# Weighted sum of two experts' outputs: tiles of 12 tokens with whole-tile vector work, and tiles of 16 tokens worked token by token

## The chip, the core and the metric

The kernel runs on one core of a Trainium2 chip. The core has several engines that run their own instruction streams side by side. Three of them matter here: VectorE (DVE in the profile), ScalarE (ACT) and SyncE (SP), which does no arithmetic and issues transfers. Transfers between the chip's memory (HBM) and the core's working memory (SBUF, 128 partitions) are carried out by 16 DMA engines, whichever engine issued them. Transfers that SP issues stand in queue q1 of the profile, those that ACT issues in q10.

The metric is device time in microseconds (us) of one execution; lower is better.

## What is computed

For each of 16 x 1024 = 16,384 tokens there are two vectors of 512 floats (the outputs of two experts) and two weights. The result is the weighted sum of the two vectors:

```python
batch, seq, hidden, n_experts, k = 16, 1024, 512, 8, 2
"expert_outputs": np.random.randn(batch, seq, k, hidden).astype(np.float32),
"combine_weights": np.random.randn(batch, seq, k).astype(np.float32),

def reference(expert_outputs, combine_weights):
    weights = combine_weights[..., np.newaxis]
    return np.sum(expert_outputs * weights, axis=2).astype(np.float32)
```

Every input element is read once and every output element written once: 67.2 MB in, 33.6 MB out. A token is 4 KB of input and 2 KB of output.

## The kernel before

The 16,384 tokens are spread over 128 partitions, so each partition owns `per` = 128 tokens. `rows` (line 34) splits them: the first `main` = 120 tokens of a partition lie next to each other in HBM, and the remaining `LAST` = 8 lie in a second block. A tile `et` (line 63) holds J = 12 tokens of each partition, both expert vectors of a token side by side: 48 KB a partition. The pool has four such buffers. The loop over g runs 11 times: ten tiles of 12 tokens and a last one of 8.

The work is done in place. `ot` (line 65) is a view of the front half of the tile's own memory, in which the sums are packed densely, so that a store reads one contiguous run of each partition. A buffer is free for a new load only when the store out of it is done.

Loads are issued by SP (line 69). The first tile is loaded in two pieces, 2 and 10 tokens; `max_dma_last_dim` cuts the first piece into rows of 4 KB. The weights `wt` are loaded once, in two pieces, by ACT (line 55). `warm` (line 60) is one small product on ACT that takes the load of ACT's function table out of the way early.

There are three forms of compute:

- Tiles 0 to 8 (lines 76 to 81): one DVE multiplication of the whole tile by the weights, repeated along each vector (`wb`), 12,288 elements a partition (line 78), then one DVE addition of the two halves, 6,144 elements (line 79). ACT issues the store (line 80).
- Tile 9 (lines 84 to 88 and 98 to 103): ACT makes the first expert's products, token by token (line 86); DVE multiplies the second expert's vectors (line 101) and adds (line 102). SP issues the store (line 103).
- Tile 10, the 8 tokens: for each token ACT makes the first product (line 86), and DVE multiplies the second vector by its weight and adds in one instruction, `scalar_tensor_tensor` (line 90). SP issues the store (line 103).

The engines are kept in step by semaphores that the framework inserts. It also sets the order in which each engine's instructions are issued, which is not always that of the source: in the profile, SP issues the last tile's load (line 69) before tile 9's store (line 103), and ACT's first product of tile 9 stands ahead of tile 8's store (line 80).

Of the kernel before, what the change touches and what calls it, by code (L numbers as in the profile page):

```python
# [1 line left out]

# [4 lines left out]


@with_exitstack
def kernel(  # L10
    ctx: ExitStack,
    tc: tile.TileContext,
    expert_outputs: bass.AP,
    combine_weights: bass.AP,
    out: bass.AP,
):

    nc = tc.nc  # L20
    b, s, k, h = expert_outputs.shape
    assert k == 2
    n = b * s
    P = nc.NUM_PARTITIONS
    per = n // P
    assert per * P == n
    J, LAST = 12, 8
    main = per - LAST
    assert main % J == 0
    eo = expert_outputs.rearrange("b s k h -> (b s) (k h)")  # L30
    cw = combine_weights.rearrange("b s k -> (b s) k")
    o = out.rearrange("b s h -> (b s) h")

    def rows(x):

        a = x[0 : P * main, :].rearrange("(p t) f -> p t f", p=P)
        b = x[P * main : n, :].rearrange("(p t) f -> p t f", p=P)
        return lambda t, c: a[:, t : t + c, :] if t < main else b[:, t - main : t - main + c, :]

    eo, cw, o = rows(eo), rows(cw), rows(o)  # L40

    dt = mybir.dt.float32
    mult = mybir.AluOpType.mult
    add = mybir.AluOpType.add
    copy = mybir.ActivationFunctionType.Copy

    last = main // J

    wpool = ctx.enter_context(tc.tile_pool(name="w", bufs=1))
    ipool = ctx.enter_context(tc.tile_pool(name="in", bufs=4))  # L50

    wt = wpool.tile([P, per * k], dt)

    for t, c in ((0, main), (main, LAST)):
        nc.scalar.dma_start(
            out=wt[:, k * t : k * (t + c)].rearrange("p (t k) -> p t k", k=k), in_=cw(t, c)
        )

    warm = wpool.tile([P, 1], dt)
    nc.scalar.activation(out=warm, in_=nc.const_aps.tensor(1.0, (P, 1), dt), func=copy)  # L60

    for g in range(last + 1):
        et = ipool.tile([P, J, k * h], dt)

        ot = et.rearrange("p j f -> p (j f)")[:, 0 : J * h].rearrange("p (j f) -> p j f", f=h)
        t0, c = g * J, J if g < last else LAST

        for a, m in ((0, 2), (2, c - 2)) if g == 0 else ((0, c),):
            nc.sync.dma_start(  # L69
                out=et[:, a : a + m],  # L70
                in_=eo(t0 + a, m),
                max_dma_last_dim=k * h * 4 if g + a == 0 else None,
            )
        if g < last - 1:

            wb = wt[:, g * J * k : (g + 1) * J * k].unsqueeze(2).to_broadcast([P, J * k, h])
            ek = et.rearrange("p j (k h) -> p (j k) h", k=k)
            nc.vector.tensor_tensor(out=ek, in0=ek, in1=wb, op=mult)  # L78
            nc.vector.tensor_tensor(out=ot, in0=et[:, :, 0:h], in1=et[:, :, h : 2 * h], op=add)  # L79
            nc.scalar.dma_start(out=o(t0, c), in_=ot)  # L80
            continue


        for i in range(c):
            t = t0 + i
            nc.scalar.activation(  # L86
                out=et[:, i, 0:h], in_=et[:, i, 0:h], func=copy, scale=wt[:, 2 * t : 2 * t + 1]
            )
            if g == last:
                nc.vector.scalar_tensor_tensor(  # L90
                    out=ot[:, i, :],
                    in0=et[:, i, h : 2 * h],
                    scalar=wt[:, 2 * t + 1 : 2 * t + 2],
                    in1=et[:, i, 0:h],
                    op0=mult,
                    op1=add,
                )
        if g < last:
            w1 = wt.rearrange("p (t k) -> p t k", k=k)[:, t0 : t0 + c, 1:2]
            x1 = et[:, :, h : 2 * h]  # L100
            nc.vector.tensor_tensor(out=x1, in0=x1, in1=w1.to_broadcast([P, c, h]), op=mult)  # L101
            nc.vector.tensor_tensor(out=ot, in0=et[:, :, 0:h], in1=x1, op=add)  # L102
        nc.sync.dma_start(out=o(t0, c), in_=ot[:, 0:c])


# [1 line left out]
_INS = ['expert_outputs', 'combine_weights']  # L107
_OUTS = [((16, 1024, 512), 'float32')]


# [23 lines left out]
```

## Time and profile before

The median of three runs is 239.04 us (239.02 to 239.04). The profiled execution has a span of 237.3 us from the first to the last instruction.

| | |
|---|---|
| median of the runs | 239.04 us |
| span of the profiled execution | 237.3 us |
| DVE multiplication of a whole tile (line 78) | 9 x 12.96 us |
| DVE addition of a whole tile (line 79) | 9 x 6.56 us |
| ACT product of one token (line 86) | 20 x 0.707 us |
| DVE multiply-add of one token (line 90) | 8 x 0.748 us |
| load of 12 tokens (6 MB), issue to landing, median | 29.9 us |
| store of 12 tokens (3 MB) from ACT, issue to landing, median | 32.7 us |
| last store (2 MB), issue to landing | 10.0 us |

A DMA transfer of a tile is cut into packets, one for each contiguous run of a partition: 128 packets, eight for each of the 16 DMA engines. The "DMA share" of the profile is the mean busy share of these 16 engines. The page also follows back a chain of waits from the last instruction; in it the DMA has 59% of the span (30% in loads, 29% in stores), DVE 33% and ACT 2%. Idle time of an engine that does not set the end costs nothing.

### The profile page before, as it was taken

The page shows a single profiled execution, that of the slowest core. Times are in us where ns is not written, and L with a number is a line of the kernel's source. Part 1 is how long each engine was busy: PE and PEld are TensorE (multiplying, and loading weights), DVE is VectorE, ACT ScalarE, POOL GpSimd, SP SyncE. Part 2 cuts the span into 40 slices and gives each one's busy share as a digit, 9 for nine tenths or more (in the row PEclk, how much of TensorE's full clock was granted, in tenths as well). Part 3 has the DMA queues.
Part 4 walks back from the last instruction along what each step waited for, and adds up shares of the span by engine and source line. Part 5 has one row for each costly group of instructions (what it writes and reads, how often), then busy time and mean ns, then how long its engine had stood idle before and what let it go on. Part 6 is the DMA issues. An engine that isn't in the chain of part 4 may idle for free.

```text
span 237.3 us, 154 instructions
## 1 busy us (share of the span) xinstructions
DVE 193.9 (82%) x28; ACT 14.0 (6%) x22; POOL 0.2 (0%) x4
## 2 busy tenths in 40 slices
DVE  0008999999999999999999879969996998785710
ACT  2000000000000000000000000000000000740800
POOL 0000000000000000000000000000000000000000
DMA  8999999989899999999897999999997979999997
GB/s 308 443 456 406 398 431 497 398 356 505 356 439 435 427 464 464 398 398 522 348 522 344 452 427 435 464 464 398 398 522 340 530 336 460 458 403 442 402 438 309
DMA packets 3728, 100.80 MB, mean 425 GB/s; under 512 B 528, under 2 KB 656, under 8 KB 912
## 3 DMA queue, kind: packets, MB, share of 16 engines
q1 hardware_dynamic: 2144, 72.35, 71.1%
q10 hardware_dynamic: 1584, 28.44, 27.9%
HBM read 67.24 MB, written 33.55 MB: 425 GB/s over the span
## 4 chain that ended last, share of the span: by engine, by line
DMA 59%; DVE 33%; ACT 2%; DVEq 0%; ACTq 0%; issue 0%; SPq 0%
DMA et<-in_expert_outputs_dram 30%; DMA out_dram<-et 29%; DVE et L78 22%; DVE et L79 11%; ACT et L86 2%; DVE et L90 1%; DVEq L129 0%; ACTq L129 0%; SPq L69 0%; DVEq L78 0%; ACTq L86 0%
## 5 line engine op out<-in xcount | busy, mean ns | idle before, releaser
L78 DVE TENSOR_TENSOR et<-et,wt 128x12288 f32<-128x12288 f32 x9 | 116.6, 12955 | 25.2 <-DMA et<-in_expert_outputs_dram 25.2
L79 DVE TENSOR_TENSOR et<-et 128x6144 f32<-128x6144 f32 x9 | 59.0, 6558 | 0.3
L86 ACT ACTIVATE et<-et,wt 128x512 f32<-128x512 f32 x20 | 12.5, 707 | 209.2 <-DMA et<-in_expert_outputs_dram 209.2
L90 DVE SCALAR_TENSOR_TENSOR et<-et,wt 128x512 f32<-128x512 f32 x8 | 5.6, 748 | 3.9 <-ACT et L86 3.7
L101 DVE TENSOR_TENSOR et<-et,wt 128x6144 f32<-128x6144 f32 x1 | 6.6, 6559 | 2.3 <-DMA et<-in_expert_outputs_dram 2.3
L102 DVE TENSOR_TENSOR et<-et 128x6144 f32<-128x6144 f32 x1 | 6.6, 6559 | 0.9 <-ACT et L86 0.9
L60 ACT ACT_TABLE_LOAD x1 | 1.3, 1283 | 1.7 <-issue 1.7
L60 ACT ACTIVATE warm<-const-float32-1.0 128x1 f32<-128x1 f32 x1 | 0.2, 202 | 0.0
L118 POOL MEMSET const-bfloat16-1.0<- 128x1 bf16 x1 | 0.1, 102 | 0.0
L118 POOL MEMSET const-uint8-127<- 128x1 uint8 x1 | 0.1, 102 | 0.0
L118 POOL MEMSET const-float32-0.0<- 128x1 f32 x1 | 0.1, 99 | 0.2 <-issue 0.2
L118 POOL MEMSET const-float32-1.0<- 128x1 f32 x1 | 0.1, 99 | 0.0
## 6 DMA issues: line engine op xcount, KB each, us to landing
et<-in_expert_outputs_dram SPq DMA_DIRECT2D x9, 6144.0 KB, 29.9
out_dram<-et ACTq DMA_DIRECT2D x9, 3072.0 KB, 32.7
et<-in_expert_outputs_dram SPq DMA_DIRECT2D x1, 5120.0 KB, 17.3
et<-in_expert_outputs_dram SPq DMA_DIRECT2D x1, 4096.0 KB, 25.1
out_dram<-et SPq DMA_DIRECT2D x1, 3072.0 KB, 14.6
out_dram<-et SPq DMA_DIRECT2D x1, 2048.0 KB, 10.0
et<-in_expert_outputs_dram SPq DMA_DIRECT2D x1, 1024.0 KB, 5.4
wt<-in_combine_weights_dram ACTq DMA_DIRECT2D x1, 120.0 KB, 4.4
```

The lines of the kernel that those rows point to most:

```text
L60: nc.scalar.activation(out=warm, in_=nc.const_aps.tensor(1.0, (P, 1), dt), func=copy)
L78: nc.vector.tensor_tensor(out=ek, in0=ek, in1=wb, op=mult)
L79: nc.vector.tensor_tensor(out=ot, in0=et[:, :, 0:h], in1=et[:, :, h : 2 * h], op=add)
L86: nc.scalar.activation(out=et[:, i, 0:h], in_=et[:, i, 0:h], func=copy, scale=wt[:, 2 * t : 2 * t + 1])
L90: nc.vector.scalar_tensor_tensor(out=ot[:, i, :], in0=et[:, i, h : 2 * h], scalar=wt[:, 2 * t + 1 : 2 * t + 2], in1=et[:, i, 0:h], op0=mul ...
L101: nc.vector.tensor_tensor(out=x1, in0=x1, in1=w1.to_broadcast([P, c, h]), op=mult)
L102: nc.vector.tensor_tensor(out=ot, in0=et[:, :, 0:h], in1=x1, op=add)
L118: nc = _bacc.Bacc("TRN2", target_bir_lowering=False, num_devices=1)
```

## The change

The tile becomes 16 tokens (64 KB a partition), and the pool has three buffers, so that the tiles take the same memory, 192 KB a partition. The loop runs 8 times, over tiles of the same size. All tiles are computed in one form, that of the old last tile: for each token one ACT product and one DVE multiply-add, both in place. A helper, `combine`, does this for c tokens from token a of the tile and returns the dense view to store.

The first tile is still loaded in two pieces, now 2 and 14 tokens, and stored in one. The last tile is loaded in pieces of 12 and 4 tokens, and each piece is computed and stored by itself. The second block of `rows` holds 16 tokens a partition in place of 8. Stores of all tiles but the last are issued by ACT, those of the last by SP.

```diff
-    J, LAST = 12, 8
-    main = per - LAST
-    assert main % J == 0
+    J = 16
+    PIECES = (12, 4)
+    assert sum(PIECES) == J and per % J == 0
+    main = per - J
...
-    ipool = ctx.enter_context(tc.tile_pool(name="in", bufs=4))
+    ipool = ctx.enter_context(tc.tile_pool(name="in", bufs=3))
...
+    def combine(et, a, c, t0):
+
+        ot = et[:, a : a + c].rearrange("p j f -> p (j f)")[:, 0 : c * h]
+        ot = ot.rearrange("p (j f) -> p j f", f=h)
+        for i in range(c):
+            t = t0 + a + i
+            x = et[:, a + i]
+            nc.scalar.activation(
+                out=x[:, 0:h], in_=x[:, 0:h], func=copy, scale=wt[:, 2 * t : 2 * t + 1]
+            )
+            nc.vector.scalar_tensor_tensor(
+                out=ot[:, i, :],
+                in0=x[:, h : 2 * h],
+                scalar=wt[:, 2 * t + 1 : 2 * t + 2],
+                in1=x[:, 0:h],
+                op0=mult,
+                op1=add,
+            )
+        return ot
+
+    last = per // J - 1
     for g in range(last + 1):
         et = ipool.tile([P, J, k * h], dt)
-
-        ot = et.rearrange("p j f -> p (j f)")[:, 0 : J * h].rearrange("p (j f) -> p j f", f=h)
-        t0, c = g * J, J if g < last else LAST
-
-        for a, m in ((0, 2), (2, c - 2)) if g == 0 else ((0, c),):
+        t0 = g * J
+        if g == 0:
+            loads, stores = ((0, 2), (2, J - 2)), ((0, J),)
+        elif g < last:
+            loads = stores = ((0, J),)
+        else:
+            loads = stores = ((0, PIECES[0]), (PIECES[0], PIECES[1]))
+        for a, c in loads:
             nc.sync.dma_start(
...
-        if g < last - 1:
-
-            wb = wt[:, g * J * k : (g + 1) * J * k].unsqueeze(2).to_broadcast([P, J * k, h])
-            ek = et.rearrange("p j (k h) -> p (j k) h", k=k)
-            nc.vector.tensor_tensor(out=ek, in0=ek, in1=wb, op=mult)
-            nc.vector.tensor_tensor(out=ot, in0=et[:, :, 0:h], in1=et[:, :, h : 2 * h], op=add)
-            nc.scalar.dma_start(out=o(t0, c), in_=ot)
-            continue
...
+        for a, c in stores:
+            ot = combine(et, a, c, t0)
+            (nc.sync if g == last else nc.scalar).dma_start(out=o(t0 + a, c), in_=ot)
```

More of the change, by code (lines that the diff above doesn't have):

```diff
@@ L45 @@
     copy = mybir.ActivationFunctionType.Copy
-    last = main // J
     wpool = ctx.enter_context(tc.tile_pool(name="w", bufs=1))
-    ipool = ctx.enter_context(tc.tile_pool(name="in", bufs=4))
+    ipool = ctx.enter_context(tc.tile_pool(name="in", bufs=3))
     wt = wpool.tile([P, per * k], dt)
-    for t, c in ((0, main), (main, LAST)):
+    for t, c in ((0, main), (main, J)):
         nc.scalar.dma_start(
@@ L69 @@
             nc.sync.dma_start(
-                out=et[:, a : a + m],
-                in_=eo(t0 + a, m),
-                max_dma_last_dim=k * h * 4 if g + a == 0 else None,
-            )
-        if g < last - 1:
-            wb = wt[:, g * J * k : (g + 1) * J * k].unsqueeze(2).to_broadcast([P, J * k, h])
-            ek = et.rearrange("p j (k h) -> p (j k) h", k=k)
-            nc.vector.tensor_tensor(out=ek, in0=ek, in1=wb, op=mult)
-            nc.vector.tensor_tensor(out=ot, in0=et[:, :, 0:h], in1=et[:, :, h : 2 * h], op=add)
-            nc.scalar.dma_start(out=o(t0, c), in_=ot)
-            continue
@@ L84 @@
[L84 to L103, printed above, removed]
+                out=et[:, a : a + c],
+                in_=eo(t0 + a, c),
+                max_dma_last_dim=k * h * 4 if t0 + a == 0 else None,
+            )
```

## The prediction

> **What bounds the kernel now.** I read the page first, and in it the DMA before the engines. DVE is busy 82% of the span, which looks like the bound; the DMA row says otherwise.
>
> ```profile
> span 237.3 us, 154 instructions
> DVE 193.9 (82%) x28; ACT 14.0 (6%) x22; POOL 0.2 (0%) x4
> DMA  8999999989899999999897999999997979999997
> DMA packets 3728, 100.80 MB, mean 425 GB/s; under 512 B 528, under 2 KB 656, under 8 KB 912
> q1 hardware_dynamic: 2144, 72.35, 71.1%
> q10 hardware_dynamic: 1584, 28.44, 27.9%
> ```
>
> The two queues together fill 71.1 + 27.9 = 99.0% of sixteen DMA engines' time: 234.9 us of 237.3. Both move bytes at one rate (72.35 MB in 0.711 x 237.3 = 168.7 us is 429 GB/s, 28.44 MB in 66.2 us is 430), so reads and writes draw on one budget. Second, I looked in the windows for where the missing 2.4 us lie.
>
> ```profile
> core 0: us, DVE busy (x) ACT busy (x) POOL busy (x), PEclk, DMA share, GB/s
> 0.00:1.00 1.00, 0.00 (x0) 0.00 (x0) 0.20 (x4) 1.00 0.00 0
> 1.00:2.00 1.00, 0.00 (x0) 0.26 (x1) 0.00 (x0) 1.00 0.40 61
> ...
> 234.00:235.00 1.00, 0.00 (x0) 0.00 (x0) 0.00 (x0) 1.00 1.07 459
> 235.00:236.00 1.00, 0.00 (x0) 0.00 (x0) 0.00 (x0) 1.00 0.62 262
> 236.00:237.00 1.00, 0.00 (x0) 0.00 (x0) 0.00 (x0) 1.00 0.00 0
> ```
>
> They lie at the two ends: nothing moves in the first microsecond nor after about 236. (Single windows scatter around 1, since a packet is counted where it ends.) Third, the timeline shows that DVE waits for the DMA in the second half, not the reverse:
>
> ```profile
> 137.66 12.96 DVE L78 TENSOR_TENSOR et<-et,wt 128x12288 f32<-128x12288 f32 x1 [2.17 <-DMA et<-in_expert_outputs_dram]
> ...
> 159.43 12.96 DVE L78 TENSOR_TENSOR et<-et,wt 128x12288 f32<-128x12288 f32 x1 [2.21 <-DMA et<-in_expert_outputs_dram]
> ...
> 217.04 9.79 SPq L103 DMA_DIRECT2D out_dram<-et  x2
> 219.93 5.01 ACT L86 ACTIVATE et<-et,wt 128x512 f32<-128x512 f32 x8 [9.51 <-DMA et<-in_expert_outputs_dram]
> 220.69 5.78 DVE L90 SCALAR_TENSOR_TENSOR et<-et,wt 128x512 f32<-128x512 f32 x8 [3.67 <-ACT et L86]
> ```
>
> Tiles start 21.77 us apart. The trace's packet records give the cause: a 49,152-byte load packet takes 1.815 us and a 24,576-byte store packet 0.912 (medians), each transfer has 128 packets, 8 per engine, and 8 x (1.815 + 0.912) = 21.82. So the kernel is a DMA stream without holes, and a change gains only by moving bytes in less time, and loses only by opening a hole.
>
> **The DMA work after the change.** Packet medians by size: 4,096 bytes 0.159 us, 16,384 0.611, 24,576 0.912, 32,768 1.213, 40,960 1.514, 49,152 1.815: each 8,192 bytes cost 0.301. My estimates from that step for sizes not in the trace: 57,344 bytes 2.116, 65,536 bytes 2.417, 8,192 bytes 0.310. Per engine:
>
> Loads before: 9 x 8 x 1.815 + 8 x 1.514 + 8 x 1.213 = 152.5 us. After: 6 x 8 x 2.417 + 8 x 2.116 + 8 x 1.815 + 8 x 0.611 = 152.4. The first two tokens (256 packets of 4,096 bytes) are the same in both.
> Stores before: 10 x 8 x 0.912 + 8 x 0.611 = 77.8. After: 7 x 8 x 1.213 + 8 x 0.912 + 8 x 0.310 = 77.7.
>
> Unrounded the two give -0.13 and -0.14: fewer, longer packets save **0.27 us**. The one size I can bound only loosely is 65,536. If such a row is cut in two, each half is 1.213 and the 48 rounds cost 48 x 0.009 = 0.4 us more; on the other side nothing under the byte rate is to be had. I take the uncut 2.417, as three equal steps in a row point to it. The weights' two small loads stay.
>
> **The compute**, costed at nothing, with the cover named. Removed are nine pairs of 12.96 + 6.56 = 19.5 us on DVE and one tile in mixed form. Added are 120 more pairs of the form that the old last tile has: 707 ns on ACT, 748 on DVE, overlapped. Eight of them took 226.47 - 219.93 = 6.5 us from the first product to the last sum, that is about 0.8 + 0.72 a token. A tile of 16 takes 0.8 + 16 x 0.72 = 12.4 us. Its cover is the tile's DMA time, 8 x (2.417 + 1.213) = 29.0 us. Without that cover, the excess over 29.0 would be paid seven times. ACT now carries products and store issues: seven stores wait in ACT's queue for the tile's last sum, and behind each stand the next tile's 16 products. Those are not due until the next load lands, some 29 us after the last one, so a wait of under a microsecond for DVE costs nothing. Four transfers fewer are issued (23 to 19, beside the weights), at about 0.34 us of SP's or ACT's time each, in which these engines would wait anyway.
>
> **Three buffers in place of four.** Both hold 48 tokens. A buffer's round is load, compute, store, and two delays. The first store, issued at 38.22, landed at 64.07 (from the trace's semaphore times): 25.85 us against 21.8 of shared packets, so about 4 us beyond; with 64 KB packets I put 6. After: 29 + 12.4 + 29 + 6 = 76 against the 3 x 29.0 = 87 that the stream needs. Before: 21.8 + 19.5 + 21.8 + 4 = 67 against 87. The spare time falls from 20 to 11 us and stays positive. The tightest place is load 3: tile 0 lands at 18.5 + 4 x 1.21 = 23.4, store 0 is issued at 34, lands at about 34 + 29 + 6 = 69, and load 2 lands at about 71. If load 3 is a little late, store 1, ready since 56, fills the engines alone for 9.7 us.
>
> **The tail** decides. If the stream has no hole, the last landing is 236.50 - 0.27 = 236.2. The two last stores hold 7.3 + 2.5 = 9.8 us, so the 4-token load and store 6 are through at 226.4. They hold 4.9 + 9.7 = 14.6 us, so if the two run side by side the 12-token load has landed by about 213. Its sums are done 0.8 + 12 x 0.72 = 9.5 later, at 222.5; a transfer needs about 1.1 us from issue to its first bytes (0.73 to 1.8 at the kernel's start), so store 12 is there at 223.6, 2.8 us before the engines would run dry. The 4-token load lands at 226.4, its sums are done 0.8 + 2.9 later, store 4 is there at 231.2, and store 12 keeps the engines busy to 233.7: 2.5 us spare. So the tail costs 0. The other bound: were store 6 half through before the 12-token load ends, that load would land 4.8 us later, at 217.7, and a hole of 2.0 us would open. I take 0, as store 6 queues behind store 5, which shares the rings with loads till near that point.
>
> **Sum.** 237.30 - 0.27 = 237.03 of span. The measured median exceeds the span by 239.04 - 237.30 = 1.74, which I carry over: **238.8 us**, 0.1% less.
>
> Two rules of the Trainium skill speak against this. The last store is 1 MiB. The nearest row is the old last store, 2 MiB, which landed 4.84 us after the store ahead of it, its packets' 8 x 0.611 and no more. The page "DMA: Bandwidth & Descriptors", section "Bandwidth", has 1 MB alone at 6.15 us, 78% of peak; by it the end would come about 3.7 us later, at 242.4. That figure is for a lone transfer, and here the ring is full. And the page "ScalarE: Activation LUTs", "Rules for kernel authors", sends multiplications to VectorE. Rows: 707 ns on ACT against 12,955 / 24 = 540 on DVE. With the rule a token would cost DVE 0.54 + 0.72 us, twelve 15.9, and store 12 would come about 3.6 us late: 242.4 too.
>
> **Rivals.**
> A, *product and sum take turns* (slower). Products and sums write into one tile, in place; were each product held until the sum before it, a token would cost 0.707 + 0.748 = 1.455 us, twelve 17.5. Store 12 would be there at 212.8 + 17.5 + 1.1 = 231.4, 5 us after the engines ran dry: 243.8. It decides from 12.3 us for the 12 tokens (1.0 a token, against 0.8 now); a milder slowing of the pairs opens the same hole in part. Against it: the eight pairs of the old last tile ran in 6.5 us and not 11.6. 15%, with the tail's other bound.
> B, *stores issued behind the next tile's products* (the issue order isn't the source's). For it: the ninth store was issued at 203.26, after the tenth tile's first product at 202.96, though its sum ended at 200.68. A store that waits for the next landing makes a buffer's round 29 + 29 + 29 + 6 = 93 against 87: up to 2 us a tile over five tiles, 248. Against: in the old kernel that delay cost the DMA nothing, and now sums end 16 us ahead of the next load. 4%.
> C, *a better stream* (faster). The packets of 49,152 average 1.823, not 1.815, as some 20 took up to 2.42 when the first store began: 1152 x 0.0084 / 16 = 0.6 us. If that vanishes, 238.2. Nothing in the change removes a first store. 20%.
> D, *64 KB rows cut in two*: 239.2, inside the forecast's class.
>
> **How the numbers follow.** About 0.2% (0.48 us) is what a measurement here tells from no change. Forecast with D: 61%, hence same 0.61; faster 0.20 from C; slower 0.19 from A and B. The likeliest time is 238.8, its own range 238.5 to 239.3. The range at 8 in 10 goes down to C's 238.2 and up to 240.6, a hole of 1.8 us in the tail, near its other bound.
>
> **What would show it.** Queue shares that again sum to 99%, DVE near 40%, DVE waiting for the DMA ahead of every tile, sums at about 0.72 us spacing, and no window under 0.8 in the last 25 us. A hole between the last load and the first tail store shows A; store issues after the next tile's first product, B. A busy sum of loads and stores below 234 us would break the byte arithmetic itself.

## The result, and the profile after

The changed kernel takes 242.25 us (median of 4 runs, 242.21 to 242.41) against 239.04 (239.02 to 239.08): 1.0136 times as long, 95% interval 1.0122 to 1.0150. It is 1.4% slower; 238.8 was forecast, and 240.6 was the upper end of the range. The profiled execution took 242.21 us with a span of 240.4, so that the span, too, grew by 3.1 us.

The page of the changed kernel, in the same lines that were read before:

```profile
span 240.4 us, 412 instructions
...
DVE 87.2 (36%) x128; ACT 81.0 (34%) x130; POOL 0.2 (0%) x4
...
DMA  9989989899999999898999999999989999999895
...
DMA packets 3155, 100.82 MB, mean 419 GB/s; under 512 B 464, under 2 KB 592, under 8 KB 848
...
q1 hardware_dynamic: 1856, 71.30, 69.4%
q10 hardware_dynamic: 1296, 29.49, 28.5%
q14 instruction: 3, 0.02, 0.0%
```

Three things are to be seen. DVE's share fell from 82% to 36%, as it should. The two data queues hold 97.9% of sixteen engines' time where they held 99.0%. And there is a queue that the page of before did not have: q14, of the kind "instruction", with three packets. Instructions, too, are fetched through the DMA engines: the kernel with 412 of them on its page has such fetches during the run, the one with 154 had none.

Then the costliest groups:

```profile
L68 DVE SCALAR_TENSOR_TENSOR et<-et,wt 128x512 f32<-128x512 f32 x128 | 87.2, 746 | 146.4 <-ACT et L65 144.6
L65 ACT ACTIVATE et<-et,wt 128x512 f32<-128x512 f32 x128 | 79.5, 708 | 149.6 <-DMA et<-in_expert_outputs_dram 149.6
```

The columns behind the bars are busy time, mean ns of one, idle time before them and what ended it. Both operations have the length forecast, and ACT stood idle for 149.6 us, all of it for loads. The compute is hidden.

The end of the timeline, with start, duration, engine, line and, in brackets, the idle time before:

```profile
205.62 0.34 ACTq L96 DMA_DIRECT2D out_dram<-et  x1
217.93 7.46 ACT L65 ACTIVATE et<-et,wt 128x512 f32<-128x512 f32 x12 [14.25 <-DMA et<-in_expert_outputs_dram]
218.68 8.43 DVE L68 SCALAR_TENSOR_TENSOR et<-et,wt 128x512 f32<-128x512 f32 x12 [13.09 <-ACT et L65]
227.13 6.86 SPq L96 DMA_DIRECT2D out_dram<-et  x2
229.74 2.56 ACT L65 ACTIVATE et<-et,wt 128x512 f32<-128x512 f32 x4 [4.36 <-DMA et<-in_expert_outputs_dram]
230.50 3.12 DVE L68 SCALAR_TENSOR_TENSOR et<-et,wt 128x512 f32<-128x512 f32 x4 [3.39 <-ACT et L65]
```

The 12-token load is in at 217.9, not 213, and its store is issued at 227.13. The windows around that (busy time of each engine, then the clock, the DMA share and GB/s):

```profile
core 0: us, DVE busy (x) ACT busy (x) POOL busy (x), PEclk, DMA share, GB/s
225.00:226.00 1.00, 1.00 (x3) 0.39 (x1) 0.00 (x0) 1.00 1.04 442
226.00:227.00 1.00, 1.00 (x2) 0.00 (x0) 0.00 (x0) 1.00 0.39 164
227.00:228.00 1.00, 0.10 (x1) 0.00 (x0) 0.00 (x0) 1.00 0.35 147
228.00:229.00 1.00, 0.00 (x0) 0.00 (x0) 0.00 (x0) 1.00 1.36 557
```

Between 226 and 228 the DMA engines are a third busy: a hole of about 1.2 us per engine. The timeline places it ahead of the arrival of the store of the 12 tokens, issued at 227.13.

So far this looks like the "other bound" of the tail. The trace's semaphore events show more. Each transfer raises its semaphore sixteen times, once for each DMA engine that has finished its part; the time of a transfer is that of the last of the sixteen. (The Trainium skill's "DMA: Bandwidth & Descriptors", "Why a DMA increments its semaphore by 16 and not by 1", says that the engines finish independently and that each posts its own increment; the sixteen separate times here agree.) Landing of the last store of each kernel, in us:

| | before | after |
|---|---|---|
| first of sixteen | 236.05 | 238.17 |
| fifteenth | 236.46 | 238.34 |
| sixteenth | 236.50 | 239.42 |

After the change, fifteen engines finish together and one 1.08 us later. The "mean of sixteen engines" that the prediction worked with hides this: one late engine sets the end, and the other fifteen only wait for it. Where that engine lost its time can be followed in the packet records and in the sixteen events of each load:

- *Fetches.* The three q14 packets of 8,192 bytes start at 84.82, 111.55 and 227.70 us and take 0.309 each; the data packet that follows each of them on its DMA engine takes 0.53, 0.24 and 0.64 us longer than its size does elsewhere. After the first, the last of the sixteen events of each load stands 0.97 us further behind the first of them (3.42 us, from 2.45). The third comes while the last load is under way, and that load's sixteenth event is 1.73 behind the fifteenth (0.87 in the load before). The second hits another engine. DVE's instruction stream, 207 entries with its waits, stands at its 71st entry at the first fetch and at its 196th at the third; ACT's at its 67th at the second. So the first and the third are taken for DVE's, the second for ACT's.
- *The start of the second ring* (a ring: the packets of one queue that wait on a DMA engine; q1 and q10 have one each). While the first store begins among loads in flight, at 34 to 44 us, 31 load packets of 65,536 bytes take 2.5 to 3.9 us in place of 2.418, 1.23 us per engine; before it was 19 to 22 packets of 49,152 and 0.56 to 0.6. And it hits engines unevenly: from then on four engines have their part of each load some 1.9 us later than the other twelve, where before all sixteen lay within 0.46. (Their part of each store comes some 1.3 us earlier; so a part of this is another order of the same work, and only the rest is lag.)
- *The byte arithmetic* gives 0.27 back, as forecast.

The trace does not name the engine of a packet, but most packets can be put in sixteen rows, as one begins where another ends. One row holds both of DVE's fetches; it has no gap up to its end at 238.99, where the other fifteen rows end between 237.84 and 237.97. For this late engine, -0.27, the two fetches with the packets behind them (0.84 and 0.95), and the difference at the ring's start (1.23 - 0.56 = 0.67 on the mean; 1.75 - 0.56 = 1.19 for its own row) make 2.2 to 2.7 of the 2.92 us by which the last landing moved. The hole is not in this sum: it shows as idle time of 0.5 to 1.9 us in the fifteen other rows, and the late one has work all through it. That fetches make one engine late and this engine sets the end was the theory (**F**, for fetch) that went into the experiments; **H**, that the hole explains the loss, was its rival.

### The profile page after: what moved, and what is told of

Same layout as the page of the kernel before. It is cut to its first block, busy times and chain, and to the rows that moved or that the text cites. A ratio compares the mean times of both kernels' runs of the same rounds, so it can differ in the third digit from the quotient of the medians.

```text
span 240.4 us, 412 instructions
## 1 busy us (share of the span) xinstructions
DVE 87.2 (36%) x128; ACT 81.0 (34%) x130; POOL 0.2 (0%) x4
## 4 chain that ended last, share of the span: by engine, by line
DMA 85%; DVE 6%; ACT 4%; issue 1%; SPq 1%; DVEq 0%; ACTq 0%
DMA et<-in_expert_outputs_dram 54%; DMA out_dram<-et 30%; DVE et L68 6%; ACT et L65 4%; SPq L89 1%; DVEq L122 0%; DVEq L68 0%; ACTq L65 0%
## 5 line engine op out<-in xcount | busy, mean ns | idle before, releaser
L68 DVE SCALAR_TENSOR_TENSOR et<-et,wt 128x512 f32<-128x512 f32 x128 | 87.2, 746 | 146.4 <-ACT et L65 144.6
L65 ACT ACTIVATE et<-et,wt 128x512 f32<-128x512 f32 x128 | 79.5, 708 | 149.6 <-DMA et<-in_expert_outputs_dram 149.6
```

The costliest lines, as they stand in the source:

```text
L65: nc.scalar.activation(out=x[:, 0:h], in_=x[:, 0:h], func=copy, scale=wt[:, 2 * t : 2 * t + 1])
L68: nc.vector.scalar_tensor_tensor(out=ot[:, i, :], in0=x[:, h : 2 * h], scalar=wt[:, 2 * t + 1 : 2 * t + 2], in1=x[:, 0:h], op0=mult, op1=add,)
```

## The experiments

The kernel before ran beside each of them. Its 90 runs there spread from 238.9 to 240.9 us (59 of them at 239.4 or less), so that the intervals, which are all against the kernel before, are wider than in the first comparison. The changed kernel itself did not run beside them, so a difference from its 242.25 has no interval.

**Is it the hole?** The last tile in pieces of 8, 4 and 4 closes it.

```diff
-    PIECES = (12, 4)
+    PIECES = (8, 4, 4)
...
-            loads = stores = ((0, PIECES[0]), (PIECES[0], PIECES[1]))
+            loads = stores = ((0, 8), (8, 4), (12, 4))
```

> The changed kernel with its last tile loaded, made and stored as 8, 4 and 4 tokens instead of 12 and 4. Theory H (a hole in the tail): in the changed kernel most DMA engines lie idle for some 0.5 to 1.6 us from about 226.5, until the store of 12 tokens arrives, which had to wait for the landing of 12 tokens and their 9 us of sums. With 8 tokens first, that store is ready some 6 us earlier and the hole closes: last landing 1.2 us earlier, about 241.0 us against 242.25. Rival F (the end is set by one DMA engine that instruction fetches have put about 1 us behind, and the idle time of the other fifteen costs nothing): no change, 242.1 to 242.4.

Measured 242.18 us (1.0112 times before, 1.0074 to 1.0151). Its windows, in the same columns:

```profile
225.00:230.00 5.00, 2.39 (x4) 1.71 (x4) 0.00 (x0) 1.00 0.98 408
230.00:235.00 5.00, 2.91 (x4) 2.12 (x4) 0.00 (x0) 1.00 0.94 400
```

The hole is gone and the time is the same. The last store lands at 239.27, its sixteenth event 0.93 behind the fifteenth. H, which expected 1.2 us less, falls: as long as an engine is late, the hole costs little or nothing. (This profile also has two losses more than that of the changed kernel: 1.46 us per engine at the ring's start in place of 1.23, and 0.19 among the short last packets at 221 to 228 us. They could hide a small gain, not one of 1.2.)

The second test put the token form alone into the kernel before: four buffers, tiles of 12, the old last tile of 8.

```diff
-        if g < last - 1:
+        if False:
...
-            if g == last:
+            if True:
...
-        if g < last:
+        if False:
...
-        nc.sync.dma_start(out=o(t0, c), in_=ot[:, 0:c])
+        (nc.scalar if g < last - 1 else nc.sync).dma_start(out=o(t0, c), in_=ot[:, 0:c])
```

> The kernel before (tiles of 12, four buffers, last tile of 8 in one piece) with every tile made token by token, a product on ACT and a multiply-add on DVE. Theory F: the longer instruction streams are fetched by DMA during the run (three 8 KB packets on the instruction queue in the changed kernel, none before), which puts one engine some 1 us behind; 239.04 + 1 = about 240, with 8 KB packets on q14 and one landing event of sixteen late. Theory H adds a hole of up to 1 us ahead of the last store of 8 tokens, since stores now leave earlier: 240 to 241. Rival (the form itself costs nothing, all of the loss is in tile size and pieces): 238.9 to 239.3.

Measured 241.60 (1.0083, 1.0052 to 1.0114), above what either expected. With the token form the first store is issued at 25.74 us in place of 38.22 and the later ones some 3 us earlier (the eighth at 175.77, before 179.01), so that more stores share the engines with the loads, and the last load lands at 226.07 (before: 219.85). Windows:

```profile
230.00:231.00 1.00, 1.00 (x3) 1.00 (x2) 0.00 (x0) 1.00 0.80 344
231.00:232.00 1.00, 1.00 (x3) 0.19 (x1) 0.00 (x0) 1.00 0.12 49
232.00:233.00 1.00, 0.71 (x2) 0.00 (x0) 0.00 (x0) 1.00 0.00 0
233.00:234.00 1.00, 0.00 (x0) 0.00 (x0) 0.00 (x0) 1.00 0.62 262
```

A hole of 2.4 us stands ahead of the last store. Here it does decide, and the landing events show how the two go together: spread over 2.15 us ahead of the hole (three fetches, at 84.5, 106.2 and 221.1), they lie within 0.17 at the end. The late engine made up its lag while the others stood idle. Here lag and hole do not add; the larger of them sets the end.

The same kernel with the last tile in two pieces of 4, which closes the hole:

```diff
+        pieces = ((0, 2), (2, c - 2)) if g == 0 else ((0, 4), (4, 4)) if g == last else ((0, c),)
+        for a, m in pieces:
...
+        for a, m in pieces if g == last else ((0, c),):
...
+            (nc.scalar if g < last - 1 else nc.sync).dma_start(out=o(t0 + a, m), in_=op)
```

> The kernel before with every tile made token by token, as in the run of the form alone, and the last tile of 8 loaded, made and stored as 4 and 4. In the run of the form alone most engines lay idle for 2.4 us ahead of the last store (its load landed at 226.07 instead of 219.85, as stores that leave 7 us earlier share the rings with it). Theory H+F: the first 4 tokens' store fills that hole, what is left is one late engine by the fetches, about 1 us: 239.8 to 240.4. Rival (the late engine alone set the end there too): no change, 241.4 to 241.7.

Measured 240.90 (1.0063, 1.0046 to 1.0080), between the two expectations. Windows:

```profile
225.00:230.00 5.00, 3.17 (x5) 2.56 (x4) 0.00 (x0) 1.00 0.98 421
230.00:235.00 5.00, 0.01 (x1) 0.00 (x0) 0.00 (x0) 1.00 0.97 411
```

No hole, 0.7 us gained, and now it is the lag that is left: sixteen events over 2.09 us, the last 1.33 behind the fifteenth. So the token form by itself costs this kernel 1.8 us (240.90 against 239.09), and the changed kernel takes 1.35 more. No run has the larger tiles with the old whole-tile work, so what the tile size costs alone is not shown.

**Is it the fetches?** First the opposite way: more instructions, with no other work.

```diff
+    junk = wpool.tile([P, 1], dt)
...
+        if 1 <= g <= 6:
+            for i in range(22):
+                nc.vector.memset(junk, 0.0)
+                if i < 10:
+                    nc.scalar.activation(out=warm, in_=warm, func=copy)
```

> The changed kernel with 132 one-element writes added on DVE and 60 one-element products on ACT, nearly all in the idle time before tile 0's second piece lands; no data moved by them. Theory F: in the changed kernel an engine's instruction fetches came some 128 of its instructions apart, so one more 8 KB fetch is due on DVE's stream and one on ACT's; each takes the same late DMA engine 0.3 us and lengthens the packet beside it by 0.2 to 0.6. 242.25 + 0.5 to 1.7 = 242.8 to 244. Rival (fetches are harmless, the late engine is late from the slow packets at the first store): 242.1 to 242.5, five fetches in the trace all the same.

Measured 242.69 (1.0125, 1.0088 to 1.0161), 0.44 more than the changed kernel, under the expectation. Five fetches instead of three, two of them before the first store: the direction of F, and less than its size. One reason may be the ring's start, which took 0.82 us per engine in this profile in place of 1.23.

Fewer instructions, in the kernel with the form and two pieces of 4: whole-tile work again in tiles 0 to 3, and in tiles 0 to 7.

```diff
+        if g < 4:
             wb = wt[:, g * J * k : (g + 1) * J * k].unsqueeze(2).to_broadcast([P, J * k, h])
```

> The run with the form alone and a last tile of 4 and 4, but with tiles 0 to 3 made by two whole-tile DVE instructions each, as in the kernel before. That run took 240.9 us with fetches at 84.5, 106.2 and 219.9 us, everything saturated, and one DMA engine 1.3 us behind the next one, of which about 0.9 came with the third fetch. 48 products and 40 DVE instructions fewer push the third fetch past the end. Theory F: two fetches are left, the last landing event loses the 0.9: 239.8 to 240.2. Rival (the late engine is late for another reason): 240.7 to 241.0.

> The same with tiles 0 to 7 whole and only tiles 8, 9 and the last made token by token: at most one fetch is left, perhaps none. Theory F: 239.0 to 239.5, the time of the kernel before, with sixteen landing events within 0.5 to 1 us at the end. Rival: the form of the last three tiles costs by itself, 240 or more.

Both 240.0 (1.0028, 1.0007 to 1.0049; and 1.0023, 1.0001 to 1.0046), 0.9 below the full form. The first lies in F's range, the second is no better than the first, a miss. Their events tell why. With four whole tiles there are two fetches, at 148.7 and 164.9, and the last store's events lie over 1.30 us; but one engine's part of a load was already 1.84 behind at 52 us, long before any fetch. (In the stores no engine stood apart, with 0.01 us between the last two events, so a part of the 1.84 is another order of the same work.) In the rows of packets it is this engine, without a fetch, that ends last, and the one with the fetch at 148.7 ends 0.34 before it: F's range was met by luck. With eight whole tiles there is one fetch in the stream, at 219.93 (DVE's 68th entry): from 86 us up to there the sixteen events lie within 0.6 us, behind it one is 0.6 us behind the fifteenth, and the last landing comes at 237.31, 0.81 later than in the kernel before. One fetch and its lengthened neighbour are 0.309 + 0.53 = 0.84. F's range allowed 0.5 more than the kernel before; the one fetch that was left costs more than that.

Fewer in the changed kernel itself, first by the old mixed form (16 ACT products, two DVE instructions on the whole tile) in tiles 0 to 5, then in tiles 0 and 1:

```diff
+    def mixed(et, t0):
...
+        for i in range(J):
+            t = t0 + i
+            nc.scalar.activation(
+                out=et[:, i, 0:h], in_=et[:, i, 0:h], func=copy, scale=wt[:, 2 * t : 2 * t + 1]
+            )
...
+        nc.vector.tensor_tensor(out=x1, in0=x1, in1=w1.to_broadcast([P, J, h]), op=mult)
+        nc.vector.tensor_tensor(out=ot, in0=et[:, :, 0:h], in1=x1, op=add)
+        return ot
...
-            ot = combine(et, a, c, t0)
+            ot = combine(et, a, c, t0) if g >= 6 else mixed(et, t0)
```

> The changed kernel with tiles 0 to 5 made by 16 ACT products and two whole-tile DVE instructions (17.5 us a tile, still under its 29 us of DMA); tiles 6 and 7 as in the changed kernel. DVE issues 84 arithmetic instructions fewer. Theory F: two of the three instruction fetches go away (those of DVE, which in the changed kernel came 128 of its instructions apart), the late engine loses at most a third of its delay: 241.2 to 241.6. Rival H alone: the tail's instructions are the same, so 242.1 to 242.4.

> The changed kernel with tiles 0 and 1 made by 16 ACT products and two whole-tile DVE instructions; all else the same, stores in the source's order. 28 DVE instructions and their waits fewer: the third fetch (227.7 us in the changed kernel) goes away. Theory F: the late engine ends about 1 us earlier, with the fifteen others at 237.9: 241.0 to 241.5. Rival: 242.1 to 242.5.

Measured 247.79 (1.0345, 1.0312 to 1.0378) and 242.70 (1.0132, 1.0088 to 1.0176): both miss, because the edit brought something else. Timeline of the first:

```profile
104.62 0.72 ACT L82 ACTIVATE et<-et,wt 128x512 f32<-128x512 f32 x1 [21.71 <-DMA et<-in_expert_outputs_dram]
104.62 8.69 DVE L87 TENSOR_TENSOR et<-et,wt 128x8192 f32<-128x8192 f32 x1 [12.98 <-DMA et<-in_expert_outputs_dram]
104.70 0.34 ACTq L109 DMA_DIRECT2D out_dram<-et  x1
```

A store is issued (104.70) behind the next tile's first product (104.62), which has waited 21.71 us for its load, while the sums were done long before. This is rival B of the prediction, and it costs 5.5 us here: with three buffers a late store means a late load, the rings run empty, and each time one starts again packets in flight slow down (1.2 to 1.7 us per engine, three times). In the second kernel the order is the source's, but the mixed form takes longer than the token form: the first store is issued at 40.87 in place of 33.52, the load ring stands empty from 69 to 78, and its new start (0.7 us per engine at 77 to 91 us) is enough to use up the gain of the missing third fetch. Neither says anything about F.

So instructions were taken off DVE without touching the order of the stores: two tokens of each long piece get both products on ACT and their sum on GpSimd.

```diff
+            if c > 8 and i in (6, 11):
+                nc.scalar.activation(
+                    out=x[:, h : 2 * h],
+                    in_=x[:, h : 2 * h],
+                    func=copy,
+                    scale=wt[:, 2 * t + 1 : 2 * t + 2],
+                )
+                nc.gpsimd.tensor_tensor(
+                    out=ot[:, i, :], in0=x[:, h : 2 * h], in1=x[:, 0:h], op=add
+                )
+                continue
```

> The changed kernel with 2 tokens of each tile (and of the piece of 12) made by two ACT products and an addition on GpSimd instead of a product and a DVE multiply-add: 16 DVE instructions and their waits fewer, all landings and stores at the times of the changed kernel within a microsecond. The third instruction fetch, which came at about the 195th instruction of DVE's stream, goes away; two are left. Theory F: the late engine loses about 1 us, 241.1 to 241.6. Rival (the late engine is the one that the first store slowed most): 242.0 to 242.6.

Measured 240.81 (1.0068, 1.0046 to 1.0090): 1.4 us less than the changed kernel, a little beyond F's range, though the kernel has more instructions in all (464 on its page). DVE's stream now ends at 191 entries, short of the 196 at which its second fetch came, and no third fetch comes before the last store has landed. That store lands at 237.65, with its sixteenth event 0.49 behind the fifteenth instead of 1.08. A part of the gain is not F's: this time the ring's start took 0.74 us per engine in place of 1.23, and left the engines within 0.7 us.

Then fetches alone in the kernel before. In the first of these runs all are early:

```diff
+    junk = wpool.tile([P, 1], dt)
+    for i in range(200):
+        nc.gpsimd.memset(junk, 0.0)
+        if i < 40:
+            nc.scalar.activation(out=warm, in_=warm, func=copy)
```

> The kernel before with 200 one-element writes on GpSimd, which is idle, and 40 one-element products on ACT before its first store; nothing else changes, no data is moved by them. Two or three instruction fetches should appear on the instruction queue. Theory F: 0.4 to 0.9 us of one engine's time for each, 239.05 + 0.5 to 1.5 = 239.5 to 240.5, and the last landing event stands apart from the other fifteen. Rival: fetches cost nothing where nothing waits for them, 239.0 to 239.2.

Measured 240.48 (1.0044, 1.0025 to 1.0063), at the upper end of F's range. From its page:

```profile
span 238.3 us, 395 instructions
...
DVE 194.0 (81%) x28; ACT 22.1 (9%) x62; POOL 19.9 (8%) x204
...
q14 instruction: 3, 0.02, 0.0%
...
L84 DVE TENSOR_TENSOR et<-et,wt 128x12288 f32<-128x12288 f32 x9 | 116.6, 12955 | 26.9 <-DMA et<-in_expert_outputs_dram 26.9
```

DVE's multiplication has the same 12,955 ns as before, so the 200 tiny GpSimd instructions do not disturb it; what is new are three fetches, at 11.5, 30.9 and 209.6. At 33.8 us, ahead of the first store, the last of sixteen landing events stood 0.98 behind the fifteenth (before: 0.15). But behind the ring's start it is 1.77 in the loads and 0.17 in the stores, and 0.58 at the end, so that two causes are mixed. The last pair of runs parts them: ACT gets tiny products that read a finished tile, behind the stores of tiles 2 to 7, so that they can't run earlier, 28 of them a tile or one.

```diff
             nc.scalar.dma_start(out=o(t0, c), in_=ot)
+            if 2 <= g <= 7:
+                for i in range(28):
+                    nc.scalar.activation(out=warm, in_=et[:, 0, 0:1], func=copy)
```

> The kernel before, with 28 one-element products on ACT behind each of the stores of tiles 2 to 7 (168 in all, about 6 us of ACT a tile at 0.2 us each, beside 21.8 us of DMA a tile). They read the tile's finished sums, so that they cannot run earlier than their place. Nothing that DVE, SP or the DMA does is changed, and ACT's own listed instructions rise from 50 to about 218. Fetch theory: ACT passes its 70th and 195th listed instruction in the middle of the stream, well after the first store's slow packets, so two fetches of 8,192 bytes appear in the instruction queue; each costs one engine 0.31 us and lengthens a neighbour by 0.24 to 0.6, the same engine both times, 1.1 to 1.8 us in all; from then on one of a load's sixteen landing events stands that far behind, and the time is 239.8 to 240.8. Rival (the lateness comes from how the ring starts, and the fetches were bystanders): fifteen and sixteen stay within 0.5 us as in the kernel before, 239.0 to 239.2.

> The control to the run before it: one such product in place of 28 behind the same six stores, so that ACT stays at about 56 listed instructions, short of its first fetch. Fetch theory: no entry in the instruction queue, landing events within 0.5 us, 239.0 to 239.2. If it is the products' place behind the stores that costs (a buffer held longer, a later store), this run is slower as well, 239.5 or more.

Medians of 12 runs: 240.00 and 239.27. Against the kernel before, the intervals (0.9987 to 1.0028 and 0.9985 to 1.0034) tell neither from it, because its own runs spread as widely. The runs themselves are more telling: with 28 products 10 of 12 lie from 239.85 to 240.12 (the others 240.40 and 240.99), with one 8 of 12 from 239.14 to 239.28 (the others 240.3 to 241.1). The main groups do not touch, and their medians lie 0.7 apart. The control's profile has no q14 line, and from the ring's start on all sixteen events within 0.5 us. That of the other:

```profile
span 239.2 us, 327 instructions
...
q14 instruction: 3, 0.02, 0.0%
```

Two of the three packets, at 102.4 and 210.0, are fetches of 8,192 bytes (the third has 32 bytes, at the very start); at each, one engine's events fall back: by 0.55 and by 0.68 us. So a fetch in mid-stream does cost its engine what F says. But this profiled execution was the slowest of the twelve, and what set its end was another engine, 1.64 us behind at 52 us, after the ring's start, which no fetch had hit. None of the ten runs of the main group was profiled; that the same two fetches set their end is inferred from the control. F is shown as a cost, and is not the whole: the ring's start can leave an engine behind by itself.

**The ring's start.** Four runs went at it: tile 0 stored in 2 and 14 tokens, so that the first store is small; the load that is in flight at the first store cut into packets of 8,192 bytes, in the changed kernel (tile 1) and in the kernel before (tile 2); and this cut added to the changed kernel with mixed form in tiles 0 and 1.

```diff
-            loads, stores = ((0, 2), (2, J - 2)), ((0, J),)
+            loads = stores = ((0, 2), (2, J - 2))
```

```diff
-                max_dma_last_dim=k * h * 4 if t0 + a == 0 else None,
+                max_dma_last_dim=k * h * 4 if t0 + a == 0 else 8192 if g == 1 else None,
```

> The changed kernel with tile 0 stored in two pieces, 2 tokens as soon as they are made (about 9 us) and then 14. Theory S (the first large store disturbs the load packets in flight: 31 packets of 65,536 bytes took 2.5 to 3.9 us instead of 2.42 between 34 and 42 us, 1.2 us for each engine; 0.6 us before): if it is a cost of the first store to the output, the small store takes it while packets are shorter, and 0.5 to 1 us is saved, 241.2 to 241.7. If it belongs to every start of a stream of stores, slow packets appear at 10 us and again at 34, and the time stays at 242.2 or rises by up to 0.5.

> The changed kernel with tile 1's load, the one in flight when the first store starts, cut into packets of 8,192 bytes instead of 65,536. Theory S' (a ring that starts against the other in flight slows about two packets of each engine by half their length): the excess between 34 and 44 us falls from 1.2 us for each engine to under 0.3, and the engines stay closer together (loads' landing events spread under 1.5 us instead of 2.5 from then on): 241.0 to 241.6. The shorter packets themselves cost 128 x 8 x 0.309 / 16 x 8 - 8 x 2.418, some 0.4 us, taken into that. Rival: the loss belongs to the store, not to the packets it meets: no gain, 242.2 to 242.8.

> The kernel before with tile 2's load, the one in flight when its first store starts, cut into packets of 8,192 bytes. Theory S': the excess between 39 and 44 us falls from 0.56 us for each engine to under 0.15; the cutting costs 0.3 us: 238.7 to 239.0, a shade faster than before. Rival: 239.0 to 239.5.

> As the last, and tile 1's load cut into packets of 8,192 bytes, which alone gave 241.99 us with the fifteen other engines done 1.9 us before the late one. If late engine and first-store loss are separate causes that add, the two remedies add once the late engine no longer hides the second: 240.2 to 241.0. If they are one cause: 241.0 to 241.5, as without the cut.

The small first store gained nothing: 242.22 (1.0112, 1.0079 to 1.0145). No load packet slowed in the first 18 us of the small store, from 22 to 40 us; packets slowed at 40 to 49, as the large store came in, and at 76 to 86, after the load ring had stood empty from 71 to 78. So the slowing does not belong to the first write; it came where large packets of one ring started beside those of the other. The cut load in the changed kernel did at the start what was hoped: 0.37 + 0.09 us per engine in place of 1.23, and fifteen engines within 0.9 us for the rest of the run. (The cutting costs 128 x 8 x 0.309 / 16 - 8 x 2.418 = 0.43 us; the product in the expectation has one factor of 8 too many.) But its median, 241.99 (1.0100, 1.0066 to 1.0134), is only 0.26 below the changed kernel's: the engine that DVE's two fetches hit ends 1.86 us behind the fifteenth, close to the 1.68 that they and their neighbours add up to in this run. In steps: its landing event stood 0.03 behind the fifteenth at 75 us, 0.86 at 97, behind DVE's first fetch, and 1.87 at 228, behind its second. In the kernel before the cut looks like a loss, 239.91 (1.0019, 1.0001 to 1.0036; all ten runs lie from 239.81 to 240.05): 62 packets slowed, 1.00 us per engine, so that smaller packets in flight did not lower the cost there. The fourth, 241.54 (1.0079, 1.0045 to 1.0112), had its packets slowed a second time, at 77 to 82 us (0.96 us per engine), and tells nothing apart.

**All three at once**: GpSimd sums, the cut load, pieces of 8, 4 and 4.

> The last kernel with tile 1's load cut into packets of 8,192 bytes and the last tile in pieces of 8, 4 and 4: third fetch, first-store loss and tail hole taken away together. If they are three causes of which the latest hides the others: 239.8 to 240.6, with two fetches left. If something else makes the changed kernel slow: 241.3 or more.

Measured 241.57 (1.0092, 1.0060 to 1.0123), slower than the GpSimd sums alone: the remedies do not add. Its profile shows that they were not all there: a third fetch came after all, at 236.76, with DVE at its 191st entry, before the last store had landed (239.43). The cut did lower the first store's loss to 0.21 us per engine, but the engines are up to 3 us apart in their events from 99 us on, and 15 packets of 16,384 bytes slow down at 224 to 228 us, among the short last transfers (0.3 us per engine). Which of these makes it slow is not shown. Why the start of a ring slows packets, and which engines it hits, stays open. No version tried beat the kernel before; of those with token work the nearest two stand at 240.0.

## Why the prediction was wrong, step by step

**What bounds the kernel**: right. It is a DMA stream before and after; in the changed kernel ACT waits for a load ahead of every tile, and DVE for ACT.

**The DMA work**: right to 0.001 us as arithmetic. Medians of 2.418 us for 65,536 bytes (2.417 forecast), 2.116 for 57,344, 0.309 for 8,192. Rows were not cut, so rival D did not occur, and the first sums of successive tiles start 29.0 us apart (but 30.0 across the first fetch, from 77.50 to 107.52). What failed is what the arithmetic was applied to: it took the sixteen engines as one stream. Rival C had the slowed packets at the first store in its hand (0.6 us), but only as a possible gain; that the larger packets would lose more there (0.74 to 1.46 us per engine in seven profiles with 65,536 bytes, 0.49 to 0.71 in eight with 49,152), and unevenly, was not asked.

**The compute, "costed at nothing"**: this step failed. Its execution is indeed hidden (a tile's 16 tokens take about 12 us of 29). But 120 token pairs more also have to be fetched, by the same DMA engines that are the bound. Three fetches of 0.309 us and the packets that they lengthen cost one engine 1.79 us and another 0.55. Page and trace of before showed no fetch during the run, so the price was not to be read there. But the trace has seven packets of 8,192 bytes and of the kind "instruction" at 8 to 11 us ahead of the first instruction, so the question "through what do the instructions come" could have been asked. The Trainium skill's "Runtime: NRT & Kernel Launch", "Instruction fetch mechanics", does say that a sequencer fetches its next block through a DMA queue of its own, and calls the cost mostly hidden. In this kernel, whose DMA engines have no gaps, it is not; and the page's blocks are of 16 KiB, where the packets here had 8,192 bytes.

**Three buffers**: right as far as it went. Stores left in source order and no load waited so long that the rings ran dry. How thin that was is seen in the mixed form with three buffers, where a late store cost 5.5 us.

**The tail, "costs 0"**: wrong, and its other bound was right, by its own mechanism: when the 12-token load landed, at 217.85 (217.7 in that bound, 213 in the one taken), 62 of store 6's 128 packets had gone. A hole opened, of 1.2 us and not 2.0, and with it the sign that the prediction had named, windows under 0.8 in the last 25 us. (Fifteen of the engines had their part of the load in by 216.99; the last 0.87 is the late engine's.) But the hole was not what cost the time, as the run with 8, 4 and 4 showed.

**Rivals A and B**: A did not occur (the twelve sums were done 9.2 us after their first product began; 9.5 was forecast). B did not in this kernel.

**The two rules against it** both came to 242.4, close to the 242.25 measured, but by luck: neither cost was there. The last store landed 2.42 us after the one ahead of it (237.00 and 239.42), its packets' 8 x 0.309 and no more, and ACT's products (708 ns each) were hidden behind loads.

**The class and the range** followed from the sum: two terms were missing from it, +1.79 for the fetches on the late engine and about +0.7 to +1.2 for the ring's start. What the runs do not settle is how much of the second is chance of the single run, since its size differs between profiles. The hole's 1.2, which the range had room for, is covered by them.

## What to carry to other kernels

Where DMA engines have no gaps, count the instructions as well as the bytes, and look for a queue of the kind "instruction" in the profile: a rewrite that replaces two large instructions by 32 small ones can be free on its engine and still be paid for in the transfers. Look at the slowest of the sixteen landing events and not only at the mean share: here one late engine set the end, and closing a hole shorter than its lag gained nothing. Treat each start of a ring beside another as a cost, and keep the rings from running empty. Don't count on the size of the packets in flight to lower that cost: with 8,192 bytes in flight it fell to 0.37 us per engine in the changed kernel and rose to 1.00 in the kernel before. A transfer's events alone can mislead, too: an engine late in the loads and early in the stores has the same work in another order.

## What the runs showed of the hardware that was not expected

- An engine's instruction stream was fetched in blocks of 8,192 bytes, mostly at about its 70th listed entry and again 120 to 136 entries later: DVE at 71 and 196, GpSimd at 77 and 202, ACT at 67 in the changed kernel, at 65 and 201 with 28 products behind six stores. (One fetch fits neither: with GpSimd sums the first came when DVE and ACT stood at entries 48 and 47.) Most blocks took 0.309 us.
- A fetch cost more than its own time. The data packet behind DVE's first fetch took 0.53 us longer in 11 of 14 profiles, whether it had 16,384, 49,152 or 65,536 bytes; the one behind a fetch of ACT took 0.24 to 0.31 us longer in all but one case. Fetches of one stream seem to fall on one DMA engine: with tile 1's load cut, DVE's two took one engine from 0.03 to 0.86 and from 0.87 to 1.87 us behind the fifteenth, and ACT's did not move it.
- When a store began beside loads in flight, packets of 65,536 bytes took up to 3.9 us in place of 2.418 for some 10 us. How much this costs differs from run to run in kernels that do the same there (1.23, 1.46 and 0.74 us per engine), and it leaves single engines behind. In one execution of the kernel before with added products this alone put one engine 1.64 us behind in the loads and 1.75 in the stores. The runs of the kernel before that take 239.8 us or more may come of the same; none of them was profiled, and this stays open.
